# A layer's latent output pair gets a fourth seven-product unit, two of them from kept sums, and two down sets are kept later

## The chip, the cores and the metric

The kernel runs on one core of a Trainium2 chip. The metric is the device time of one execution in microseconds; the median of three runs before the change is 1445.47 us (1445.11 to 1447.64). TensorE (PE) multiplies matrices, VectorE (DVE) and ScalarE (ACT) work element by element, GpSimd (POOL) and SyncE (SP) issue most of the transfers (DMA).

## The reference

One layer of a decoder on 256 tokens of width 2048, all in float32:

```
h = rms_norm(x);  P = h @ w_in                    # queries, latents, keys, values, two gates
A = latent attention (16 heads);  B = sliding-window attention (32 heads)
merged = sigmoid(gA) * (A @ w_o_mla) + sigmoid(gB) * (B @ w_o_swa)
x = x + rms_norm(merged @ w_out)
a, b = split(rms_norm(x) @ ffn_w_up)              # 2 x 5632 columns
x = x + rms_norm((gelu(causal_conv3(a)) * b) @ ffn_w_down)
```

## The kernel before

Every weight is used once, so it is read from memory in pieces of 128x1024 (a row of 128 input features), split and multiplied. A number is kept as a high part `whi` (ScalarE's cast, line 161) and a low part `wlo` (VectorE's subtraction, line 162), and each product is three matmuls: high by high, high by low, low by high (`mm3`, lines 196 to 198). So one piece costs one load on SP's queue into a raw slot, one cast, one subtraction, and its matmuls.

`pair_gemm` multiplies 1024 output columns at a time. It takes the input rows in pairs. A plain pair ("p" in an order string) makes 8 block products, 24 matmuls of 512 columns. A seven-product pair makes 7 (21 matmuls), in the manner of Strassen's and Winograd's scheme: it needs four sums of weight blocks and four sums of activation blocks (`token_sums`, `a_sums`). For "o" the weight sums are made on the spot by four VectorE subtractions (`weight_sums`, line 230). For "s" with `parked` they have been kept: `park_sums` loads the two rows on POOL's queue into a staging tile (line 244), subtracts in four steps (`less`, line 252), stores them to memory (lines 257, 262), and `seven_parked` later loads the sums like any weight. Behind the last seven-product pair `end_sums` adds the product sums up in one ScalarE copy and four VectorE sums (lines 364 to 371).

Time is counted in ticks: `tick()` runs what was put down for this step by `at`, and a piece or two of weights go by per tick. Within this a scheduler sets the order of each engine's instructions by priority; `keep_in_program_order` and `high_priority` bind or lift single ones. Each engine then works through its queue in order.

The stages, with their place in the profile: the first products, sliding-window attention, gates and the sliding-window output; the latent attention (up to 545 us); the latent output, `a_pair` for columns 0 to 1023 (545 to 587 us) and plain products for the rest; `w_pair` and plain products for `w_out` (633 to 709 us); up-projection, a first part of the down-projection, the rest of the up-projection; at last `db` and `dc`, the last down pairs (from 1341 us). In `dc` the second tokens' products of seven pieces are held back to the end. Each finished block of the result passes `z_block`: a sum, a ScalarE square, and a scaling by the norm's gain (line 1523), which may be put off to a later tick. `A_ORDER` is "ppopopop": five plain pairs, three made on the spot. In the latent attention six sets of sums are kept: `tc0` for `dc`, and `ta0` to `ta4` for the first down part. The others are kept in the up-projection's stage.

Of the kernel before, what the change touches and what calls it, by code (L numbers as in the profile page):

```python
# [19 lines left out]
P = 128  # L20
# [20 lines left out]
def trunk_layer(ctx, tc, x, x_cols_in, conv_cols_in, g_mix_post, g_ffn_post, w_in, w_q, w_kv,  # L41
# [136 lines left out]
    def at(t, *fs):  # L178
        steps[max(t, now[0])].extend(fs)
# [56 lines left out]
    def park_sums(name, w, k, c0, place, t0, lead=5):  # L236

        td = [dram.tile([P, 1024], F32, name=f"{name}{i}") for i in range(2)]
        st = []

        def load():
            rows, tag = place(f"{name}s")
            for i in range(2):
                ins = pool.dma_start(rows[i], w[(k + i) * P:(k + i + 1) * P, c0:c0 + 1024])
                if tag not in staged:
                    tc.keep_in_program_order(ins)
            staged.add(tag)
            st.extend(rows[i][:, j * 512:(j + 1) * 512] for i in range(2) for j in range(2))
            st.extend(rows)

        def less(o, x, y):
            tc.keep_in_program_order(vec.tensor_tensor(st[o], st[x], st[y], op=ALU.subtract))

        def even():
            less(0, 1, 0)
            less(1, 3, 1)
            pool.dma_start(td[0], st[4])

        def odd():
            less(3, 3, 0)  # L260
            less(2, 2, 3)
            pool.dma_start(td[1], st[5])

        at(t0 - lead, load)
        at(t0, even)
        at(t0 + 1, odd)
        return td
# [9 lines left out]
    def pair_gemm(name, w, k0, c0, order, act_of, s_of, kind, d, place=None, sums=None, parked=None, held=None, into=None, tied=False, urgent=True):  # L277
# [80 lines left out]
        def end_sums():  # L358
            q1, q5, q7, q6 = q
            d0, d1, d2, d3 = d() if callable(d) else d  # L360

            def first_sums():
                with tc.high_priority(200) if urgent else nullcontext():
                    act.copy(d0, q1)
                    vec.tensor_tensor(d1, d0, q6, op=ALU.add)
                    vec.tensor_tensor(d2, d1, q7, op=ALU.add)

            def more_sums():
                with tc.high_priority(200) if urgent else nullcontext():
                    vec.tensor_tensor(d3, d2, q5, op=ALU.add)  # L370
                    vec.tensor_tensor(d1, d1, q5, op=ALU.add)

            at(now[0], first_sums)
            at(now[0] + 1, more_sums)

        plain_of, seven_of, spot_of = iter(range(n, len(order))), iter(range(n)), iter(range(order.count("s"), n))
        for i, kd_ in enumerate(order):
# [649 lines left out]
        at(t0 + 6, lambda: pt(0), lambda: pt(1))  # L1027
        at(t0 + 7, lambda: pv(0), lambda: pv(1))

    parked_b2.append(park_sums("tc0_", w_down, 24, 1024, stage, now[0] + 7))  # L1030
    parked_a = [park_a(i, stage, now[0] + 13 + 6 * i) for i in range(EARLY)]
    b = now[0] + 2
    for u in range(8):
        if u % 4 == 0:
# [69 lines left out]
            at(now[0] + later + t, load)  # L1104

    as_ = {}
    as_tiles = []

    def a_sums(u):
        if u % 2 == 0:  # L1110
            as_tiles.append(sb(p3, [P, D], f"as{u // 2}", F32R, tag=f"x2_{u // 2}"))
        o = u % 2 * 1024
        tmp = sb(base, [P, 1024], f"at{u}", tag="rx")
        as_[u] = token_sums(at_[u].bitcast(F32), tmp[:, 0:512], tmp[:, 512:1024],
                            as_tiles[u // 2][:, o:o + 512], as_tiles[u // 2][:, o + 512:o + 1024])
# [12 lines left out]
    def a_pair():  # L1128
        halves = [sb(p6, [P, 1024], f"l{n}1", tag="f" + n, bufs=2) for n in "ab"]
        lds = [merge_loads(0, 8), [[x_[:, t * 512:(t + 1) * 512] for x_ in halves] for t in range(NT)]]  # L1130
        for t in range(NT):
            merge_load(*lds[1][t], 1, t, 11)
        gp = sb(p6, [P, D], "araw", tag="gp")
        more_raw[:] = [raw_of, raw_f, raw_of, lambda name: gp[:, 0:1024], raw_of, raw_f, lambda name: gp[:, 1024:2048]]
        c = pair_gemm("a", wo_a, 0, 0, A_ORDER, lambda k, t: (AH(k)[:, t * P:(t + 1) * P], AL(k)[:, t * P:(t + 1) * P]),
                      lambda u: as_[u], 0, ud_place, tied=True)
        more_raw.clear()
        turn.update(raw=0)

        def pair_evac(i):  # L1140
            t, j = divmod(i, 2)
            vec.tensor_tensor(ud_a[i], ud_a[i], c[i], op=ALU.add)
            merged(*lds[j][t], ud_a[i])

        for n_, i in enumerate((0, 2, 1, 3)):
            at(now[0] + n_, lambda i=i: pair_evac(i))
        for p in range(4):
            at(now[0] + 3 + p, lambda p=p: m_cols(p, lds[p // 2]))

    for u in range(NA_):  # L1150
        at(now[0] + 3 * u, lambda u=u: a_sums(u))
    for i in range(4, 12):
        at(now[0] + 36 + 2 * i, lambda i=i: late_loads(i))
    turn_flex("raw")
# [78 lines left out]
    def w_pair():  # L1233
# [10 lines left out]
        for i in range(4):  # L1244
            at(now[0] + i, lambda i=i: pair_evac(i))

    w_pair()
    es4.close()
    es8, p8 = open_pool("p8")
# [320 lines left out]
    def pair_end(i):  # L1570
        t, j = divmod(i, 2)
        vec.tensor_tensor(dsum[t][j], dsum[t][j], ud[i], op=ALU.add)
        z_block(c_db[i], j, t, now[0] + (8 if t == 0 else 14))

    a_raw = lambda k: lambda name: a_tile(name, k)
    more_raw[:] = [raw_of, a_raw(2), raw_of, a_raw(3), raw_of, a_raw(6), a_raw(7)]
# [26 lines left out]
        unpark(i // 4, i % 4)  # L1603
    for i in range(4):
        t, j = divmod(i, 2)
        vec.tensor_tensor(dsum[t][2 + j], dsum[t][2 + j], ud2[i], op=ALU.add)
    z_block(c[0], 2, 0)
    z_block(c[1], 3, 0)
    z_pre(0)
# [24 lines left out]


RING = 4
A_ORDER = "ppopopop"
NA_ = A_ORDER.count("o")
GATE_ORDER = "ppspspsp"
OUT_ORDER = "ppsppspp"  # L1640
B_ORDER = "pospsspssp"
# [76 lines left out]
```

## Time and profile before

| | |
|---|---|
| median of three runs | 1445.47 us |
| the profiled execution | 1445.55 us |
| its span, first to last instruction | 1443.8 us |
| PE busy | 1432.9 us (99%) |
| DVE busy | 1206.8 us (84%) |
| ACT busy | 877.1 us (61%) |
| mean granted clock of TensorE | 0.998 |

Busy times are those of one execution under the profiler. Matmuls overlap: one of 512 columns is shown with 0.39 us, but they follow each other faster, so the pace is read from the starts. VectorE's steps overlap a little as well. A row of the order in time has the start, the length, the engine, the line, what is written and read, and in brackets how long the engine had been idle and who ended that.

### The profile page before, as it was taken

To read this page: it belongs to the slowest core of one execution; us is meant where nothing else is said; L and a number is where in the kernel's file an instruction comes from. 1 tells how busy PE (TensorE), PEld (TensorE's weight loads), DVE (VectorE), ACT (ScalarE), POOL (GpSimd) and SP (SyncE) were. 2 spreads that over 40 slices of the span, in tenths; PEclk is the share of its full clock that TensorE was granted. 3 is DMA by queue.
4 is the path that set the end of the run, shared out by engine and by line. 5 is a ranking of instruction groups with operands and counts; after the bars stand their busy time and mean duration, and the time that the engine had idled before them with its cause. 6 is when DMAs were issued, how large, how long until landed. Compare 5 with 4: busy or idle time off the path is not lost.

```text
span 1443.8 us, 21415 instructions
## 1 busy us (share of the span) xinstructions
PE 1432.9 (99%) x7479; PEld 1225.0 (85%) x7479; DVE 1206.8 (84%) x2106; ACT 877.1 (61%) x1414; POOL 112.7 (8%) x224
## 2 busy tenths in 40 slices
PE   9999999999999999999999999999999999999997
PEld 8888888888888888888888888888888888888886
DVE  7789898988777777979799988987989698877798
ACT  7589875554555655455666555556756465555673
POOL 2001000000000111100000111100000110110000
PEclk9999999999999999999999999999999999999999
DMA  9755475657876777866776999877888889878975
GB/s 309 212 177 154 110 251 199 214 180 227 255 213 205 240 235 264 303 234 220 224 253 210 312 326 329 310 262 236 326 289 316 302 294 305 273 265 279 342 254 215
DMA packets 162315, 365.44 MB, mean 253 GB/s; under 512 B 21008, under 2 KB 32144, under 8 KB 162208
## 3 DMA queue, kind: packets, MB, share of 16 engines
q1 hardware_dynamic: 138192, 278.82, 58.4%
q0 software_dynamic: 23872, 85.00, 17.3%
q8 instruction: 58, 0.95, 0.3%
q14 instruction: 49, 0.40, 0.1%
q10 hardware_dynamic: 144, 0.26, 0.1%
HBM read 327.29 MB, written 36.75 MB: 252 GB/s over the span
## 4 chain that ended last, share of the span: by engine, by line
PE 95%; DVE 2%; ACT 1%; issue 1%; DMA 1%; DVEq 0%; ACTq 0%
PE ub L1407 10%; PE ua L1407 10%; PE accg L196 8%; PE accg L198 8%; PE accg L197 8%; PE ub L1411 5%; PE ua L1411 5%; PE cd L198 2%; PE cd L196 2%; PE cd L197 2%; PE cg L196 2%; PE cg L198 2%; PE cg L197 2%; PE qd L198 1%; PE qd L196 1%; PE qd L197 1%
## 5 line engine op out<-in xcount | busy, mean ns | idle before, releaser
L161 ACT CAST whi<-raw 128x1024 fp32r<-128x1024 f32 (+2 forms) x494 | 497.6, 1017 | 332.7 <-PE accg L198 78.1
L162 DVE TENSOR_TENSOR wlo<-raw,whi 128x1024 fp32r<-128x1024 f32 (+2 forms) x494 | 574.5, 1176 | 119.6 <-ACT whi L161 114.3
L1407 PE MATMUL ua<-ahl,whi 128*128 128x512 f32 x640 | 154.6, 391 | 0.0
L1407 PE MATMUL ub<-ahl,whi 128*128 128x512 f32 x640 | 154.5, 391 | 0.0
L196 PE MATMUL accg<-whi,ahl 128*128 128x512 f32 (+1 forms) x352 | 137.3, 391 | 0.0
L1407 PEld LDWEIGHTS ua<-ahl,whi 128*128 128x128 f32 x640 | 117.6, 188 | 22.7
L1407 PEld LDWEIGHTS ub<-ahl,whi 128*128 128x128 f32 x640 | 117.6, 188 | 22.7
L198 PE MATMUL accg<-whi,ahl 128*128 128x512 f32 (+1 forms) x352 | 136.0, 386 | 0.0
L197 PE MATMUL accg<-wlo,ahl 128*128 128x512 f32 (+1 forms) x352 | 135.5, 385 | 0.0
L1411 PEld LDWEIGHTS ub<-ahl,wlo 128*128 128x128 f32 x640 | 82.2, 191 | 3.2
L1411 PEld LDWEIGHTS ua<-ahl,wlo 128*128 128x128 f32 x640 | 82.2, 191 | 3.1
L1411 PE MATMUL ua<-ahl,wlo 128*128 128x256 f32 x640 | 83.7, 283 | 0.0
L1411 PE MATMUL ub<-ahl,wlo 128*128 128x256 f32 x640 | 83.2, 283 | 0.0
L198 PEld LDWEIGHTS accg<-whi,ahl 128*128 128x128 f32 x352 | 66.1, 188 | 12.6
L196 PE MATMUL accg<-whi,bhl 128*128 128x512 f32 x192 | 76.1, 396 | 0.0
L198 PE MATMUL accg<-whi,bhl 128*128 128x512 f32 x192 | 75.2, 391 | 0.0
L197 PEld LDWEIGHTS accg<-wlo,ahl 128*128 128x128 f32 x352 | 66.2, 188 | 10.4
L197 PE MATMUL accg<-wlo,bhl 128*128 128x512 f32 x192 | 75.1, 391 | 0.0
L196 PEld LDWEIGHTS accg<-whi,ahl 128*128 128x128 f32 x352 | 66.1, 188 | 10.4
L162 DVE TENSOR_TENSOR wlo<-xraw,whi 128x1024 fp32r<-128x1024 f32 x33 | 40.3, 1220 | 12.9 <-ACT whi L161 12.6
L161 ACT CAST whi<-xraw 128x1024 fp32r<-128x1024 f32 x33 | 34.8, 1054 | 24.5 <-PE ub L1407 14.2
L198 PEld LDWEIGHTS accg<-whi,bhl 128*128 128x128 f32 x192 | 36.1, 188 | 7.6
(757 smaller groups left out, 2947.8 us busy)
## 6 DMA issues: line engine op xcount, KB each, us to landing
raw<-in_ffn_w_up_dram SPq DMA_DIRECT2D x143, 512.0 KB, 5.3
raw<-in_w_in_dram SPq DMA_DIRECT2D x99, 512.0 KB, 4.5
raw<-in_ffn_w_down_dram SPq DMA_DIRECT2D x61, 512.0 KB, 6.0
xraw<-in_ffn_w_up_dram SPq DMA_DIRECT2D x33, 512.0 KB, 5.7
ta_s<-in_ffn_w_down_dram POOLq DMA_DIRECT2D x32, 512.0 KB, 6.3
ta<-ta_s POOLq DMA_DIRECT2D x32, 512.0 KB, 5.5
raw<-ta SPq DMA_DIRECT2D x32, 512.0 KB, 5.5
raw<-in_w_o_swa_dram SPq DMA_DIRECT2D x28, 512.0 KB, 4.8
```

What stands on the lines that cost most here:

```text
L161: act.copy(hi[:, a:b], raw[:, a:b])
L162: vec.tensor_tensor(lo[:, a:b], raw[:, a:b], hi[:, a:b].bitcast(F32), op=ALU.subtract)
L196: pe.matmul(o, ah, bh, start=start, stop=False)
L197: pe.matmul(o, ah, bl, start=False, stop=False)
L198: pe.matmul(o, al, bh, start=False, stop=stop)
L1407: pe.matmul(acc[i], hi[:, c], hn[p][:, j * 512:(j + 1) * 512], start=p + j == 0, stop=stop)
L1411: pe.matmul(acc[i][:, 0:256], lo[:, c], hn[p][:, j * 512:j * 512 + 256], start=False, stop=False)
```

## The change

The latent output's pair goes from "ppopopop" to "pposposp": four plain pairs and four seven-product pairs, of which two load kept sums (`parked_w`, made in the latent attention ahead of `tc0`) and two make them on the spot. The token sums of the four are made in the order in which the pairs come. Two of the five early down sets are no longer made in the latent attention but beside `w_pair`. Apart from that, the sums behind the last pair, `dc`, which is the one without `urgent`, come three ticks later and are bound to program order, and the scalings of `db`'s blocks come at 6 and 9 ticks instead of 8 and 14.

```diff
@@ end_sums @@
+            def add(o, x_, y):
+                ins = vec.tensor_tensor(o, x_, y, op=ALU.add)
+                if not urgent:
+                    tc.keep_in_program_order(ins)
...
-            at(now[0], first_sums)
-            at(now[0] + 1, more_sums)
+            at(now[0] + (0 if urgent else 3), first_sums)
+            at(now[0] + (1 if urgent else 4), more_sums)
@@ the latent attention @@
-    parked_b2.append(park_sums("tc0_", w_down, 24, 1024, stage, now[0] + 7))
-    parked_a = [park_a(i, stage, now[0] + 13 + 6 * i) for i in range(EARLY)]
+    parked_w = [park_sums(f"tw{i}_", wo_a, 2 * i, 0, stage, now[0] + 7 + 6 * i) for i in range(2)]
+    parked_b2.append(park_sums("tc0_", w_down, 24, 1024, stage, now[0] + 19))
+    parked_a = [park_a(i, stage, now[0] + 25 + 6 * i) for i in range(EARLY - 2)]
@@ a_pair @@
-                      lambda u: as_[u], 0, ud_place, tied=True)
+                      lambda u: as_[u], 0, ud_place, parked=parked_w, tied=True)
...
-    for u in range(NA_):
-        at(now[0] + 3 * u, lambda u=u: a_sums(u))
+    for u, t in ((2, 0), (0, 3), (3, 6), (1, 9)):
+        at(now[0] + t, lambda u=u: a_sums(u))
@@ the w_out stage @@
+    for i in range(2):
+        parked_a.append(park_a(EARLY - 2 + i, stage, now[0] + 13 + 7 * i))
     w_pair()
@@ the last down pairs @@
-        z_block(c_db[i], j, t, now[0] + (8 if t == 0 else 14))
+        z_block(c_db[i], j, t, now[0] + (6 if t == 0 else 9))
...
-        vec.tensor_tensor(dsum[t][2 + j], dsum[t][2 + j], ud2[i], op=ALU.add)
+        tc.keep_in_program_order(vec.tensor_tensor(dsum[t][2 + j], dsum[t][2 + j], ud2[i], op=ALU.add))
@@ the tables @@
-A_ORDER = "ppopopop"
-NA_ = A_ORDER.count("o")
+A_ORDER = "pposposp"
```

What stands in VectorE's queue before the change where `w_pair` ends: the splits of the last two weight sums (`yg`), of the last plain pair's two rows and of the next columns' pieces (`raw`), and the sums of the pair's products (lines 365 to 371, `qw`).

```order
L162 TENSOR_TENSOR wlo_7102<-yg_1_6407,whi_7101 128x1024
L162 TENSOR_TENSOR wlo_7113<-yg_1_6409,whi_7112 128x1024
L162 TENSOR_TENSOR wlo_7125<-raw_7122,whi_7124 128x1024
L162 TENSOR_TENSOR wlo_7147<-raw_7144,whi_7146 128x1024
L365 TENSOR_TENSOR yg_0_6406<-yg_0_6406,qw_6921 128x512
L162 TENSOR_TENSOR wlo_7173<-raw_7170,whi_7172 128x1024
L366 TENSOR_TENSOR yg_0_6408<-yg_0_6406,qw_6920 128x512
L162 TENSOR_TENSOR wlo_7196<-raw_7193,whi_7195 128x1024
L370 TENSOR_TENSOR yg_0_6408<-yg_0_6408,qw_6919 128x512
L371 TENSOR_TENSOR yg_0_6406<-yg_0_6406,qw_6919 128x512
```

And in the changed kernel, where the sums have line 363 and the subtractions of the first moved down set (`ta_s`) line 252:

```order
L162 TENSOR_TENSOR wlo_7135<-yg_1_6424,whi_7134 128x1024
L252 TENSOR_TENSOR ta_s<-ta_s 128x512
L162 TENSOR_TENSOR wlo_7150<-raw_7147,whi_7149 128x1024
L252 TENSOR_TENSOR ta_s<-ta_s 128x512
L363 TENSOR_TENSOR yg_0_6421<-yg_0_6421,qw_6940 128x512
L252 TENSOR_TENSOR ta_s<-ta_s 128x512
L363 TENSOR_TENSOR yg_0_6423<-yg_0_6421,qw_6939 128x512
L252 TENSOR_TENSOR ta_s<-ta_s 128x512
L363 TENSOR_TENSOR yg_0_6423<-yg_0_6423,qw_6938 128x512
L363 TENSOR_TENSOR yg_0_6421<-yg_0_6421,qw_6938 128x512
L162 TENSOR_TENSOR wlo_7175<-raw_7172,whi_7174 128x1024
L162 TENSOR_TENSOR wlo_7204<-raw_7201,whi_7203 128x1024
```

The split of the last plain row (`raw_7144` before, `raw_7172` now) stood directly behind the one before it; now four subtractions and four sums are between them.

TensorE's queue at the same place in the changed kernel, from the last plain row's first matmul (`whi_7174`, `wlo_7175`) on; `accg` are the next columns:

```order
L196 MATMUL cw_6835<-whi_7174,ahl_6024 128x512
L196 MATMUL cw_6836<-whi_7174,ahl_6024 128x512
L196 MATMUL cw_6837<-whi_7174,ahl_6024 128x512
L196 MATMUL cw_6838<-whi_7174,ahl_6024 128x512
L196 MATMUL accg_0_7199<-whi_7203,ahl_6017 128x512
L196 MATMUL accg_1_7200<-whi_7203,ahl_6017 128x512
L197 MATMUL cw_6835<-wlo_7175,ahl_6024 128x512
L198 MATMUL cw_6835<-whi_7174,ahl_6024 128x512
```

Before, the order there was 196, 197, 198 for each block; now six matmuls that need no `wlo` of this row come ahead of the first that does.

VectorE's queue in `dc` before the change, from the split of a kept sum to the last pieces' splits; `L1523` is a scaling of a `db` block, `L1606` the sum with the pair's product sums (`ue`), `L365` to `L371` these sums:

```order
L162 TENSOR_TENSOR wlo_14425<-raw_14422,whi_14424 128x1024
L1523 TENSOR_TENSOR ds_0_10868<-ds_0_10868,gpost_0_13637 128x512
L162 TENSOR_TENSOR wh_14439<-raw_14436,wh_14438 128x1024
L1523 TENSOR_TENSOR ds_0_10868<-ds_0_10868,gpost_0_13637 128x512
L1606 TENSOR_TENSOR ds_1_11401<-ds_1_11401,ue_14434 128x512
L365 TENSOR_TENSOR ue_14434<-ue_14434,qdc_14153 128x512
L162 TENSOR_TENSOR wlo_14454<-raw_14451,whi_14453 128x1024
L366 TENSOR_TENSOR ue_14435<-ue_14434,qdc_14152 128x512
L162 TENSOR_TENSOR wlo_14468<-raw_14465,whi_14467 128x1024
```

And in the changed kernel (`L1531` is the scaling, `L363` the sums):

```order
L162 TENSOR_TENSOR wlo_14417<-raw_14414,whi_14416 128x1024
L1531 TENSOR_TENSOR ds_0_10905<-ds_0_10905,gpost_0_13674 128x512
L162 TENSOR_TENSOR wlo_14430<-raw_14427,whi_14429 128x1024
L162 TENSOR_TENSOR wlo_14442<-raw_14439,whi_14441 128x512
L162 TENSOR_TENSOR wlo_14451<-raw_14448,whi_14450 128x1024
L1531 TENSOR_TENSOR ds_0_10905<-ds_0_10905,gpost_0_13674 128x512
L162 TENSOR_TENSOR wlo_14464<-raw_14461,whi_14463 128x1024
L162 TENSOR_TENSOR wh_14478<-raw_14475,wh_14477 128x1024
L162 TENSOR_TENSOR wlo_14490<-raw_14487,whi_14489 128x1024
L162 TENSOR_TENSOR wlo_14502<-raw_14499,whi_14501 128x1024
L162 TENSOR_TENSOR wlo_14514<-raw_14511,whi_14513 128x1024
L363 TENSOR_TENSOR ue_14473<-ue_14473,qdc_14190 128x512
```

Behind the split into `wh` the next splits now follow directly; the scalings stand further up, and the first of the sums comes behind three more splits.

## Rows read from the trace of the kernel before

**Rows 1.** The page's head: span; busy us, share of the span and instructions.

```profile
span 1443.8 us, 21415 instructions
...
PE 1432.9 (99%) x7479; PEld 1225.0 (85%) x7479; DVE 1206.8 (84%) x2106; ACT 877.1 (61%) x1414; POOL 112.7 (8%) x224
```

**Rows 2.** PE's waits: whom it waited for, us in total, times, longest.

```profile
PE warm L74 <- DVE ramp L65: 1.1, 1, 1.1
PE cdc L197 <- DVE wlo L162: 0.9, 1, 0.9
```

**Rows 3.** PE in order of time at the end.

```profile
1417.23 0.39 PE L196 MATMUL cdc<-whi,bhl 128*128 128x512 f32 x1
1418.54 0.50 PE L197 MATMUL cdc<-wlo,bhl 128*128 128x512 f32 x1 [0.92 <-DVE wlo L162]
...
1426.47 0.39 PE L198 MATMUL cdc<-wh,bhl 128*128 128x512 f32 x1
...
1434.85 0.28 PE L198 MATMUL zb<-whi,ghl 128*128 128x256 f32 x1
```

**Rows 4.** PE in order of time, the last plain pair of w_pair.

```profile
670.28 0.39 PE L196 MATMUL cw<-whi,ahl 128*128 128x512 f32 x1
...
675.72 0.39 PE L196 MATMUL accg<-whi,ahl 128*128 128x512 f32 x1
```

**Rows 5.** DVE in order of time, start of the latent output's pair.

```profile
547.20 1.23 DVE L162 TENSOR_TENSOR wlo<-araw,whi 128x1024 fp32r<-128x1024 f32 x1 [1.42 <-ACT whi L161]
549.35 1.22 DVE L162 TENSOR_TENSOR wlo<-raw,whi 128x1024 fp32r<-128x1024 f32 x1 [0.92 <-ACT whi L161]
```

**Rows 6.** ACT in order of time, the down pair db.

```profile
1365.75 1.05 ACT L161 CAST whi<-raw 128x1024 fp32r<-128x1024 f32 x1 [1.67 <-PE cdb L198]
```

**Rows 7.** Stretches: length, busy us of PE, PEld, DVE, ACT, POOL; PEclk, DMA share, GB/s.

```profile
545.00:590.00 45.00, 45.00 (x201) 37.25 (x199) 36.90 (x45) 24.10 (x26) 3.85 (x8) 1.00 0.79 276
...
633.00:675.00 42.00, 42.00 (x190) 34.76 (x190) 35.79 (x44) 22.87 (x25) 2.67 (x5) 1.00 0.55 175
675.00:715.00 40.00, 39.95 (x178) 32.79 (x178) 29.80 (x41) 22.39 (x31) 0.07 (x1) 1.00 0.72 236
```

**Rows 8.** DVE in order of time, end of w_pair.

```profile
661.43 0.68 DVE L230 TENSOR_TENSOR yg<-mr3hi 128x512 f32<-128x512 f32 x1
662.03 0.69 DVE L230 TENSOR_TENSOR yg<-mr3lo,mr3hi 128x512 f32<-128x512 f32 x1
...
666.85 1.22 DVE L162 TENSOR_TENSOR wlo<-yg,whi 128x1024 fp32r<-128x1024 f32 x1 [1.20 <-ACT whi L161]
668.21 1.23 DVE L162 TENSOR_TENSOR wlo<-raw,whi 128x1024 fp32r<-128x1024 f32 x1
669.64 1.23 DVE L162 TENSOR_TENSOR wlo<-raw,whi 128x1024 fp32r<-128x1024 f32 x1 [0.20 <-ACT whi L161]
```

**Rows 9.** DVE in order of time at the end.

```profile
1411.30 2.50 DVE L162 TENSOR_TENSOR wlo<-raw,whi 128x1024 fp32r<-128x1024 f32 x2 [0.93 <-ACT whi L161]
...
1414.33 1.22 DVE L162 TENSOR_TENSOR wh<-raw,wh 128x1024 fp32r<-128x1024 f32 x1
...
1417.26 1.22 DVE L162 TENSOR_TENSOR wlo<-raw,whi 128x1024 fp32r<-128x1024 f32 x1
...
1434.99 0.75 DVE L1518 TENSOR_TENSOR z<-ds,zb 128x256 f32<-128x256 f32 x2
```

**Rows 10.** POOL in order of time, latent attention.

```profile
481.14 0.54 POOL L262 DMA_DIRECT2D ta<-ta_s  x1 [3.77 <-DVE ta_s L252]
486.08 1.06 POOL L244 DMA_DIRECT2D ta_s<-in_ffn_w_down_dram  x2 [4.40 <-DMA ta<-ta_s]
```

**Rows 11.** The staging tile's transfers, loads and stores together.

```profile
DMA to landing us min/median/max: 2.9/6.2/8.7
```

**Rows 12.** ACT in order of time, dc.

```profile
1410.22 1.05 ACT L161 CAST whi<-raw 128x1024 fp32r<-128x1024 f32 x1 [1.69 <-DMA raw<-tc]
```

More of the change, by code (lines that the diff above doesn't have):

```diff
@@ L364, in first_sums @@
                     act.copy(d0, q1)
-                    vec.tensor_tensor(d1, d0, q6, op=ALU.add)
-                    vec.tensor_tensor(d2, d1, q7, op=ALU.add)
+                    add(d1, d0, q6)
+                    add(d2, d1, q7)
             def more_sums():
                 with tc.high_priority(200) if urgent else nullcontext():
-                    vec.tensor_tensor(d3, d2, q5, op=ALU.add)
-                    vec.tensor_tensor(d1, d1, q5, op=ALU.add)
-            at(now[0], first_sums)
-            at(now[0] + 1, more_sums)
+                    add(d3, d2, q5)
+                    add(d1, d1, q5)
+            at(now[0] + (0 if urgent else 3), first_sums)
+            at(now[0] + (1 if urgent else 4), more_sums)
         plain_of, seven_of, spot_of = iter(range(n, len(order))), iter(range(n)), iter(range(order.count("s"), n))
@@ L1106, in trunk_layer @@
     as_ = {}
-    as_tiles = []
+    as_tiles = {}
     def a_sums(u):
-        if u % 2 == 0:
-            as_tiles.append(sb(p3, [P, D], f"as{u // 2}", F32R, tag=f"x2_{u // 2}"))
+        if u // 2 not in as_tiles:
+            as_tiles[u // 2] = sb(p3, [P, D], f"as{u // 2}", F32R, tag=f"x2_{u // 2}")
         o = u % 2 * 1024
```

## The prediction

> **What bounds the kernel now.** I read the page's head first: the span is 1443.8 us and TensorE (PE) is busy for 1432.9 us of it [rows 1]. The 10.9 us left are 1.1 us ahead of the first warm-up matmul [rows 2], 0.9 us in one wait on VectorE (DVE) near the end [rows 2], and the 8.7 us behind the last matmul, which starts at 1434.85 us and takes 0.28 [rows 3]. So the second view is PE's waits, which has these two rows and no other [rows 2]: TensorE is the bound from the first product to the last, and any other engine matters only where it makes PE wait. Its pace comes from the order in time: from 670.28 to 675.72 us 24 matmuls of 512 columns start, 0.2267 us each [rows 4]; the one of the wait starts 1.31 us after the one before it [rows 3]. The reader is to see that VectorE, though busy for 84% of the span [rows 1], is paced by PE for nearly all of it: its idle time ends with ScalarE's cast [rows 5], and that cast ends its own wait when PE gives back a weight slot [rows 6].
>
> A change is therefore worth the matmuls it takes away, less the waits it brings to PE, plus what happens in the tail, where PE is done and DVE's queue alone is left.
>
> **The change part by part.**
>
> *One plain pair of rows becomes a seven-product pair.* `A_ORDER` had five plain pairs (24 matmuls each) and three sevens (21); it now has four and four. Three matmuls of 512 columns go: 3 x 0.2267 = 0.68 us [rows 4], all of it on the path, since PE has no gap in this stage (45.00 us busy of 45.00 [rows 7]). Value -0.68; I see no reason for more or less.
>
> *What feeds that stage.* DVE's work in it hardly changes: a seven-product pair costs three subtractions of 1024 columns and one of 512 where a plain one costs two of 1024 (+1.14 + 0.60 us), and a fourth token sum comes (some 2 us: two steps at 0.60 and four small ones at about 0.2), against which the 4 weight sums of one on-spot unit fewer go (4 x 0.60). The fourth token sum is issued between two weight splits, where DVE waits 1.42 and 0.92 us for ScalarE [rows 5]: hidden; without that cover it is 2 us earlier work in a queue that is several microseconds ahead, still nothing. The two kept units now read their sums by DMA through the same seven raw slots. The nearest row is the down stage, which runs kept units through seven slots as well: there the casts wait for PE, not for a DMA [rows 6]. Value 0, bounds 0 to +1.3.
>
> *The attention stage* made six kept sets (one for the last down columns, five down sets) and makes six now (two of `w_o_mla`, that one, three down sets), at the same places of DVE's and POOL's queues, four subtractions, two loads and two stores each. 0.
>
> *Two down sets go into the w_out stage.* This is 8 new subtractions of 128x512 on DVE, 4 loads and 4 stores on the POOL queue. The first set's four land in the worst place, inside the last 10 us of the pair, between the split of the last weight sum and the split of the last plain row. I work it out on the clock of before. That split of the last sum starts at 666.85 and the next can start 1.14 later, at 667.99 [rows 8]. In front of the split of the last plain row there used to be one split; now there are one split, the four new subtractions and all four sums of the pair's products, which the new order puts ahead of it (first two excerpts of the order, in the section on the change): 1.14 + 8 x 0.60 = 5.94 us. The pitch of 0.60 is that of neighbouring 512-column steps, 661.43 to 662.03 [rows 8]. So the split starts at 673.93 instead of 669.64 [rows 8] and ends 1.23 later, at 675.16. PE wants it, in the new order, after 12 matmuls of the row before, four high products and two of the next columns brought forward: 670.28 + 18 x 0.2267 = 674.36 us [rows 4]. It is late by 0.80, with 0.06 us of hand-off (split ends 1418.48, matmul starts 1418.54 [rows 3, 9]) 0.86 us. What a wait costs PE beyond its first gap is seen at the one wait before: the gap is 1.08 us over the pitch, but the 35 matmuls from 1417.23 to 1426.47 take 9.24 instead of 7.93 us, 1.31 in all [rows 3]. By that ratio 0.86 becomes 1.04. Value +1.0. The bounds: with one step less in the way it is +0.3, and PE cannot gain from added work; with eight steps that follow each other at their whole 0.68 us [rows 8], 0.64 us more, it is (0.86 + 0.64) x 1.21 = +1.8.
>
> The Trainium skill (VectorE: DVE Perf Modes, § The DRAIN you can't avoid) says that a VectorE step does not begin until the one before has emptied the pipe. The trace does not agree: steps that take 0.68 us follow each other at 0.60 [rows 8]. By that rule this term would be its upper bound, and the sum +0.7 instead of -0.1 us.
>
> After that the queue recovers: each chunk of the next columns gives PE 12 matmuls, 2.72 us, against 1.14 for its split and 1.2 for two sums, so the second set's four steps, one ahead of each of four later splits, fall into a growing lead. They wait for a load, though: POOL issues it once the first set's store has landed, 4.4 us behind the end of the store's issue, as between 481.14 + 0.54 and 486.08 [rows 10]. From the end of the fourth subtraction, 672.8, that gives a load at 678.3, and with the median landing of 6.2 us [rows 11] its second half at 685.0, against about 685.6 when DVE gets there. Value 0; the upper end is the second rival.
>
> *The sums of the last pair come three steps later, and the scaling of the finished blocks earlier.* Before, three 0.60 us steps (one `L1523`, one `L1606`, one `L365`) stand between the split that ends at 1415.5 and the one that starts at 1417.26, for which PE waits [rows 9]. Now they are out of its way: of the four scalings three come before the gap in which DVE waits to 1411.30 for a late load (0.93 us idle [rows 9]; the cast waited 1.69 us [rows 12]). The split PE waited for can then end at 1416.5 instead of 1418.48, and PE wants it at 1417.46: the wait goes, PE ends 1.31 us sooner. What is late next is DVE: its queue runs densely from there to the last blocks, whose sum starts at 1434.99 [rows 9], while PE's last matmul is over at 1435.13 [rows 3]; so the tail gains only what DVE gains, one 0.60 us step moved into the idle 0.93. Part of that is lost again, because the first two scalings delay the return of raw slots by up to 0.8 us while loads are the limit. Value -0.4; bounds +0.2 and -1.3 (PE's whole gain).
>
> **Sum:** -0.68 + 1.0 - 0.4 = -0.1 us. The profiled execution took 1445.55 us (span plus 1.75), 0.08 above the median; so 1445.5 us.
>
> **The rivals.**
>
> *No new wait, and the whole tail.* If DVE reaches the last plain row in time, 1.0 us is not paid, and if the end follows PE, the tail gives 1.31: -0.68 - 0.6 to -1.31, 1443.6 to 1444.3. For it: the splits of before are ready 2.4 us ahead of PE there (669.64 + 1.23 against 673.23). Against it: 4.3 us are put in front. Chance 0.18.
>
> *The second set's load comes late, and the kernel is slower.* The first of its subtractions waits on DVE for that load, and the split of the sixth chunk of the columns stands behind it; PE wants that at 675.72 + 5 x 2.72 + 0.23, with the 1.0 us of the first wait 690.6 [rows 4]. A store and a load at the longest landing, 8.7 us each [rows 11], put the load at 691.2 and the split's end 1.8 us later, at 693.0: 2.5 us of gap on top, 3.0 by the ratio above, 1448.5. It decides from a landing after 688.7. For it: the landings' spread, 2.9 to 8.7; against it: the median leaves 3.7 us. Chance 0.08.
>
> *Loads short on the raw slots.* The added 4.2 MB share the engines with the weights: 175 GB/s at a share of 0.55 is 318 at full, so 13 us of all engines in a stretch of 40 that is used to 0.72 [rows 7], 11 us free. Splits there are up to 6 us ahead of PE once the columns run, which speaks against it, and two stages would have to fail alike for more. One late raw, its cast as late as the one of [rows 12] (1.69 us) less some 0.4 of lead, is +1.3, in this stage or in that of the latent output: 1446.8. The Trainium skill (DMA: Bandwidth & Descriptors, § Issuing engines are not separate DMA queues) says that transfers of all issuing engines run on the same 16 and interleave; no row here shows how much one queue's landings slow another's. Chance 0.12.
>
> **How the numbers follow.** Forecast 0.62 (its own range 1444.4 to 1446.6), then 0.18, 0.08 and 0.12. A measurement of this kernel tells apart about 0.2%, 2.9 us: faster means under 1442.6, slower over 1448.4. Only the far end of the first rival and a loss that I don't see reach the one: 0.05. The second rival's upper half, and the third together with the forecast's upper bounds, reach the other: 0.09. Same: 0.86. The range, 1443.7 to 1447.6, takes in the first and third rival and leaves out most of the second.
>
> **What would show it.** Right: one wait of PE on a split in the w_out pair near 673 us, 0.7 to 1.0 us; no wait near 1416; three matmuls fewer (7476 records, if none is missing); the pair of the latent output 0.7 us shorter; the tail from the first block's sum to the end unchanged in length, and shorter in all by under 0.7. Wrong: no wait at 673 (first rival); waits at 690 behind a load (second); casts that wait for raw loads while PE stands (third). A time beyond 2.9 us on either side means a mechanism that is not in this list.

## The result, and the profile after

The changed kernel takes 1453.41 us (median of 6 runs, 1452.63 to 1455.12), the kernel before beside it 1445.68 (6 runs, 1444.87 to 1447.70). The ratio is 1.0057, with an interval from 1.0046 to 1.0067: 7.7 us slower. The forecast was 1445.5 us and its range ended at 1447.6; it was wrong.

The head of the page after, where [rows 1] stood before:

```profile
span 1450.8 us, 21452 instructions
...
PE 1434.5 (99%) x7476; PEld 1224.2 (84%) x7476; DVE 1213.8 (84%) x2118; ACT 878.9 (61%) x1417; POOL 116.8 (8%) x232
```

Three matmuls are gone, and yet the span is 7.0 us longer. PE's waits (whom it waited for, us in total, times, longest) say where, against the two rows of before [rows 2]:

```profile
PE accg L197 <- DVE wlo L162: 2.2, 3, 0.8
PE accg L196 <- DVE uda L363: 1.8, 1, 1.8
PE warm L74 <- DVE ramp L65: 1.1, 1, 1.1
PE accg L196 <- ACT whi L161: 0.8, 2, 0.5
PE cw L197 <- DVE wlo L162: 0.6, 1, 0.6
PE x2T L1209 <- DVE x L1206: 0.4, 1, 0.4
PE acckv L197 <- DVE wlo L162: 0.3, 1, 0.3
```

The wait at the end of `dc` is gone. New are one in the latent output (`uda`), the predicted one on a split in `w_pair` (`cw`), and five behind it in the last columns of `w_out` (`accg`), with a short one (`x2T`) after these; the one of 0.3 us (`acckv`) is among the first products. In order of time on PE, with the last matmul, which started at 1434.85 before [rows 3]:

```profile
586.82 0.39 PE L198 MATMUL accg<-whi,bhl 128*128 128x512 f32 x1
588.97 0.50 PE L196 MATMUL accg<-whi,bhl 128*128 128x512 f32 x1 [1.76 <-DVE uda L363]
...
676.79 0.50 PE L197 MATMUL cw<-wlo,ahl 128*128 128x512 f32 x1 [0.63 <-DVE wlo L162]
...
703.92 0.39 PE L198 MATMUL accg<-whi,ahl 128*128 128x512 f32 x1
704.62 0.49 PE L196 MATMUL accg<-whi,ahl 128*128 128x512 f32 x1 [0.32 <-ACT whi L161]
705.88 0.50 PE L197 MATMUL accg<-wlo,ahl 128*128 128x512 f32 x1 [0.77 <-DVE wlo L162]
...
714.84 0.50 PE L197 MATMUL accg<-wlo,ahl 128*128 128x512 f32 x1 [0.68 <-DVE wlo L162]
...
1441.71 0.28 PE L198 MATMUL zb<-whi,ghl 128*128 128x256 f32 x1
```

By the starts the first stall costs 2.15 - 0.23 = 1.9 us, and the one at 676.79 a gap of 1.07, that is 0.84 beyond the pitch. Seven gaps follow between 703.92 and 714.84, in a stretch where PE had stood for 0.05 us of 40 before [rows 7]. The same stretches after:

```profile
545.00:590.00 45.00, 43.24 (x191) 35.48 (x190) 36.83 (x45) 26.33 (x29) 3.77 (x7) 1.00 0.89 314
633.00:675.00 42.00, 42.00 (x190) 34.77 (x190) 35.73 (x45) 22.41 (x26) 3.52 (x7) 1.00 0.56 182
675.00:715.00 40.00, 36.21 (x151) 27.55 (x151) 28.94 (x33) 19.04 (x27) 3.44 (x7) 1.00 0.87 305
```

PE loses 1.76 us in the first and 3.8 in the third, where the engines of the DMA are now busy to 0.87 instead of 0.72. That share looks like the cause; the experiments show that VectorE's added steps bring most of the loss without the sets' own transfers, at a share of 0.76.

The same matmuls in both profiles show where the time goes. The first one of `w_pair` starts at 633.26 us before and at 634.86 after, the first of `ua` in the up stage at 767.45 and 775.57, and PE's last at 1434.85 and 1441.71. An earlier matmul, at 535.79 and 536.01, is 0.22 us apart already; less that, the change is 1.38 us behind at the start of `w_pair`, 7.90 at that of `ua` and 6.64 at the end.

**The stall at 588.97.** `accg` is the second accumulator of the next columns; its bank was one of the pair's and is free when the last two product sums (L363) are done. These two stand on DVE behind a split that waits for a cast:

```profile
586.49 1.23 DVE L162 TENSOR_TENSOR wlo<-raw,whi 128x1024 fp32r<-128x1024 f32 x1 [2.70 <-ACT whi L161]
587.63 1.28 DVE L363 TENSOR_TENSOR uda<-uda,qa 128x512 f32<-128x512 f32 x2
```

and the cast waits on ACT for a load:

```profile
585.41 3.19 ACT L161 CAST whi<-raw 128x1024 fp32r<-128x1024 f32 x3 [4.25 <-DMA raw<-in_w_o_mla_dram]
```

It is the load of the columns' second chunk, the third of the column loads in SP's queue. SP issues it at 578.70, just as the split that empties its slot ends (it starts at 577.45 and takes about 1.23). In SP's order of time:

```profile
578.70 0.37 SPq L140 DMA_DIRECT2D raw<-in_w_o_mla_dram  x1
```

The view by line, cut to this one load, gives its landing:

```profile
DMA to landing us min/median/max: 6.6/6.6/6.6
```

Before the change the same load was issued at 576.78 and landed sooner:

```profile
576.78 0.37 SPq L140 DMA_DIRECT2D raw<-in_w_o_mla_dram  x1
```

```profile
DMA to landing us min/median/max: 4.5/4.5/4.5
```

The slots follow a cycle of seven (`more_raw`). The pair took 22 of them before and takes 24 now, so at its end the cycle stands two places further, and the last pieces sit in other slots. The next columns use only the five of the ring, and find them free later.

### The profile page after: what moved, and what is told of

It reads as the page before. It is cut to its first block, busy times and chain, and to the rows that moved or that the text cites. A ratio compares the mean times of both kernels' runs of the same rounds, so it can differ in the third digit from the quotient of the medians.

```text
span 1450.8 us, 21452 instructions
## 1 busy us (share of the span) xinstructions
PE 1434.5 (99%) x7476; PEld 1224.2 (84%) x7476; DVE 1213.8 (84%) x2118; ACT 878.9 (61%) x1417; POOL 116.8 (8%) x232
## 4 chain that ended last, share of the span: by engine, by line
PE 93%; DMA 3%; DVE 2%; ACT 1%; issue 0%; SPq 0%; DVEq 0%; ACTq 0%
PE ub L1415 10%; PE ua L1415 10%; PE accg L196 7%; PE accg L198 7%; PE accg L197 7%; PE ub L1419 5%; PE ua L1419 5%; DMA raw<-in_w_out_dram 2%; PE cd L196 2%; PE cd L198 2%; PE cd L197 2%; PE cg L198 2%; PE cg L196 2%; PE cg L197 2%; PE qd L196 1%; PE qd L198 1%
```

## The experiments

Each is compared with runs of the kernel before on the same chip (medians 1445.0 to 1445.5). The last column is a length read from each profile: from one and the same matmul near the end of the latent attention (it starts at 535.79 us before and at 536.01 after) to the start of PE's last. What lies ahead of it varies by up to 1.7 us between these profiles and does not enter. It is one execution each, and for e4_up_ring, e5_transfers, e6_subs and e7_one one of the two fastest.

| kernel | median us | ratio [interval] | PE's length us |
|---|---|---|---|
| before | 1445.68 | 1 | 899.06 |
| after | 1453.41 | 1.0057 [1.0046, 1.0067] | 905.70 |
| e1_tail | 1445.67 | 1.0005 [0.9996, 1.0014] | 897.78 |
| e2_up | 1448.73 | 1.0027 [1.0017, 1.0038] | 902.06 |
| e3_ring | 1450.28 | 1.0034 [1.0022, 1.0046] | 903.12 |
| e4_up_ring | 1445.23 | 0.9998 [0.9990, 1.0007] | 897.05 |
| e5_transfers | 1446.44 | 1.0007 [0.9999, 1.0016] | 897.12 |
| e6_subs | 1450.31 | 1.0042 [1.0029, 1.0056] | 901.41 |
| e7_one | 1447.13 | 1.0017 [1.0008, 1.0026] | 899.09 |
| e8_wide | 1458.98 | 1.0096 [1.0082, 1.0110] | 912.10 |
| e9_phase | 1450.77 | 1.0037 [1.0025, 1.0050] | 904.72 |
| e10_old_tail | 1445.23 | 0.9998 [0.9989, 1.0007] | 899.78 |
| e11_pool | 1445.43 | 1.0002 [0.9993, 1.0011] | 898.11 |
| e12_again | 1445.98 | 1.0005 [0.9996, 1.0014] | 897.32 |
| e13_early | 1449.40 | 1.0026 [1.0017, 1.0035] | 901.39 |

**e1_tail: the end's edits alone, on the kernel before.**

```diff
-            at(now[0], first_sums)
-            at(now[0] + 1, more_sums)
+            at(now[0] + (0 if urgent else 3), first_sums)
+            at(now[0] + (1 if urgent else 4), more_sums)
-        z_block(c_db[i], j, t, now[0] + (8 if t == 0 else 14))
+        z_block(c_db[i], j, t, now[0] + (6 if t == 0 else 9))
```

> The kernel before with the edits of the last pair alone (its sums three steps later, the finished blocks scaled earlier). Theory: the wait of TensorE near 1417 us was all that stood between the last loads and the end, so TensorE's last matmul starts 1.3 us sooner and the whole is 1.2 us shorter, 1444.5. As predicted: VectorE's queue sets the end, -0.4 us, 1445.3. If the edits are worth nothing by themselves: 1445.7.

PE's length is 1.28 us shorter, and the wait near 1417 is gone. DVE's last four steps start 2.99 us behind PE's last matmul (2.82 before), so 1.11 of it reaches DVE's end (PE's last starts at 1434.00, DVE's four in this row):

```profile
1436.99 2.74 DVE L1557 SCALAR_TENSOR_TENSOR ds<-ds,rz,x2b 128x512 f32<-128x512 f32 x4
```

The time shows none of it: the interval allows 0.6 us at most. In the profiled execution the slowest of the last stores took 3.2 us to land instead of 2.2, about as much as the gain. Whether that belongs to the edit or to chance is open.

**e2_up: the two sets in the up stage, on the kernel after.**

```diff
-    for i in range(2):
-        parked_a.append(park_a(EARLY - 2 + i, stage, now[0] + 13 + 7 * i))
-    for i in range(sum(NA) - EARLY):
-        parked_a.append(park_a(i + EARLY, second_stage if i % 2 else stage, now[0] + 9 + UP_STEP * i // 2, lead=9))
+    for i in range(sum(NA) - EARLY + 2):
+        parked_a.append(park_a(i + EARLY - 2, second_stage if i % 2 else stage, now[0] + 9 + UP_STEP * i // 2, lead=9))
-UP_STEP = 11
+UP_STEP = 9
```

> The kernel after with its two down sets of the w_out stage made in the up stage instead, with the other eleven (step 9 for 11, so that the last comes at the same place). Theory: these two sets alone make the stalls between 675 and 722 us (1.0 + 5.2 + 0.6), which go; the one at 586.8 (2.1) stays: 1453.4 - 6.8 = 1446.6. Rival, that the late loads of the latent pair carry on into the w_out stage: part of the stalls at 704 to 715 stays, 1448 or more. Rival, that the up stage has no room for 13 sets: new waits there.

Every wait between 675 and 722 us is gone; the one at 587 stays, and this time it is 3.0 us. The up stage takes 13 sets without a wait in this profile. Behind this longer stand PE's granted clock is 0.50 (from 592 to 594 us), and eight matmuls start 0.427 us apart instead of 0.227; against e4_up_ring, which has no such stand, PE's length is 5.01 us longer. The eight runs lie between 1446.3 and 1452.2; that the stall's size makes this spread is likely, but only one of them was profiled.

**e3_ring: the phase of the cycle mended, on the kernel after.**

```diff
-        more_raw[:] = [raw_of, raw_f, raw_of, lambda name: gp[:, 0:1024], raw_of, raw_f, lambda name: gp[:, 1024:2048]]
+        g0, g1 = (lambda name, i=i: gp[:, 1024 * i:1024 * i + 1024] for i in range(2))
+        seven = [raw_of, raw_f, raw_of, g0, raw_of, raw_f, g1]
+        more_raw[:] = seven + seven + [raw_of, raw_f] + seven + [raw_of]
```

> The kernel after with one edit: two entries more in the cycle of raw slots of the latent pair (24 instead of 7 repeated), so that its last two pieces sit in the same slots as before the change and the loads of the next columns find theirs free one or two pieces sooner. Theory: the stall at 586.8 is the phase of that ring; it goes, -2.1 us, 1451.4. Rival, that the kept sums' four more loads or the kept unit itself make the cast late, whatever the slots: the stall stays, 1453.4.

The stall at 587 is gone, PE's length is 2.58 us shorter, and what is left of PE's waits, but for 0.3 us among the first products, is the `w_out` stage:

```profile
PE accg L197 <- DVE wlo L162: 2.0, 3, 0.8
...
PE accg L196 <- ACT whi L161: 0.7, 2, 0.4
PE cw L197 <- DVE wlo L162: 0.6, 1, 0.6
```

But the expectation's reason was half right: the second chunk's load is issued hardly sooner (578.85, in a profile that is 0.65 us later), it lands sooner, in 4.3 us instead of 6.6. Behind it come loads at 579.99 and 582.26; in the kernel after they came at 580.07, 581.49 and 583.23. So the phase spreads the slots' release. That the wider spacing is what makes the load land sooner was not tested apart.

**e4_up_ring: both edits.** The diffs are those of e2_up and e3_ring.

> Both edits together, on the kernel after. Theory: no wait of over 0.5 us is left, and the sum is that of the parts: 1445.7 - 0.7 (three matmuls) - 1.2 (the end) = 1443.8. If one of the stalls has another cause: 1446 to 1447.

PE waits nowhere in the stages that the change touches:

```profile
PE warm L74 <- DVE ramp L65: 1.1, 1, 1.1
PE acckv L526 <- ACT whi L161: 0.3, 1, 0.3
```

Its length is 2.01 us under the kernel before: 0.68 for the three matmuls and 1.28 for the end make 1.96. So the losses are these two and no others. In the order taken here they are 2.58 for the ring's phase and 903.12 - 897.05 = 6.07 for the two sets. In the other order the phase is 902.06 - 897.05 = 5.01 and the sets 3.64, because the stand of e2_up is longer and the clock falls behind it. The median is that of before all the same.

**e5_transfers and e6_subs: the halves of the sets.** Both add to e4_up_ring, in the `w_out` stage, sets whose results nothing reads; the first has only the DMAs, the second only the subtractions, on rows filled by GpSimd.

```diff
+        def load():
...
+                pool.dma_start(rows[k], w_down[(2 * (i + 3) + k) * P:(2 * (i + 3) + k + 1) * P, 0:1024])
...
+        def even():
+            pool.dma_start(td[0], st[4])
+        def odd():
+            pool.dma_start(td[1], st[5])
```

and, in the second:

```diff
+                pool.memset(rows[k], 0.0)
...
+        def even():
+            less(0, 1, 0)
+            less(1, 3, 1)
+        def odd():
+            less(3, 3, 0)
+            less(2, 2, 3)
```

> The kernel without waits (both edits: sets in the up stage, ring phase mended) and, added to it, only the transfers of two down sets in the w_out stage, at the places where the change put them: four loads and four stores of 0.5 MB on POOL's queue, no subtraction (the stores go to a place that nothing reads). Theory: the stalls at 704 to 715 come from loads of w_out that land later beside these transfers, so they are here: +4 to +6, 1449 to 1451; no wait at 675. Rival: VectorE's added steps make them; then this is 1445.2 as without.

> The same kernel without waits and, added to it, only the eight subtractions in the w_out stage, on rows that POOL fills with zeros instead of loading them; no transfer, and nothing reads the results. Theory: the wait of TensorE near 675 us is these steps' (+1.0) and nothing at 704 to 715: 1446.2. Rival: the subtractions delay the weight splits, with them the return of the raw slots and the loads; stalls at 704 to 715, 1449 or more.

The theory of e5_transfers was not put to the test. Its run takes PE's length up by 0.07 us only, but the scheduler, with no subtraction to wait for, put its transfers into the stage before: the last of them goes out at 619.90, where the change has its four stores and the second set's two loads from 672.30 to 697.33. In POOL's order of time, first e5_transfers, then the kernel after:

```profile
619.90 0.54 POOL L1273 DMA_DIRECT2D tx<-tx_s  x1 [1.38 <-DMA tx_s<-in_ffn_w_down_dram]
```

```profile
678.33 1.06 POOL L244 DMA_DIRECT2D ta_s<-in_ffn_w_down_dram  x2 [3.08 <-DMA ta<-ta_s]
```

The stretch from 675 to 715 us says the same, in e5_transfers, e6_subs and e3_ring (the last two numbers are the DMA engines' share and GB/s; e4_up_ring has 0.70 and 234):

```profile
675.00:715.00 40.00, 39.95 (x179) 32.67 (x178) 29.81 (x42) 22.56 (x32) 0.55 (x1) 1.00 0.70 237
```

```profile
675.00:715.00 40.00, 38.33 (x163) 29.93 (x162) 29.56 (x40) 19.78 (x29) 1.08 (x2) 1.00 0.76 255
```

```profile
675.00:715.00 40.00, 36.73 (x153) 28.32 (x154) 28.61 (x32) 18.58 (x27) 3.19 (x6) 1.00 0.87 299
```

So what the transfers alone cost at their place is not known. In e6_subs the subtractions do stand where the change has them, and its theory fell: without the sets' own transfers they cost 4.4 us, bring back both stalls, and lengthen the loads of `w_out` issued between 668 and 700 to a median of 6.7 us, against 4.8 in e4_up_ring. The run is not wholly free of added transfers: the next set's two loads, at 595 in e4_up_ring, go out on POOL's queue at 692.29 and 692.83 here, since the staging tile is in use until then. The first 1.0 us, at 674.61, comes before them; what they add to the rest was not told apart. SP's issues of e6_subs show how. They come at 692.95, 694.04 and 695.18, and the next only after 7 us:

```profile
695.18 0.37 SPq L140 DMA_DIRECT2D raw<-in_w_out_dram  x1
...
702.17 0.37 SPq L140 DMA_DIRECT2D raw<-in_w_out_dram  x1
```

e4_up_ring issues at 687.30, 689.87, 692.21, 694.28 and 696.72, one per chunk. Here the split of the last plain row starts at 673.34 instead of 669.06, 4.3 us later. The slots come back late, three at once, their loads are on the way together and land after 6.8 to 7.0 us, and nothing is issued until these are split. ACT then waits 6.45 us:

```profile
699.84 1.05 ACT L161 CAST whi<-raw 128x1024 fp32r<-128x1024 f32 x1 [6.45 <-DMA raw<-in_w_out_dram]
```

This falls into the columns where only one token tile is multiplied ahead, so PE takes a chunk in 1.36 us instead of 2.72, and the lead is used up at 704. With subtractions and transfers together (e3_ring) it is 1.7 us more, and the rows show the transfers at work: loads that go out at 677.45 and 679.82 in e6_subs land after 7.1 and 6.7 us; those that go out at 677.34 and 679.71 in e7_one, behind the next set's two loads on POOL's queue at 675.98 and 676.50, land after 9.7 and 9.3.

**e7_one: only the first of the two sets.**

```diff
+    parked_a.append(park_a(EARLY - 2, stage, now[0] + 13))
     w_pair()
```

> The kernel without waits with one of the two sets, the first, back in the w_out stage (the other one in the up stage). Theory: the wait at 675 is back (+1.0); the first set's stores and loads are over by 680, so the last columns are fed as before: 1446.2. If one set's transfers are enough to put the raw ring behind: 1448 or more.

PE's length is 2.04 us longer than without: the gap at 673.44 is again 1.07, and one of 0.98 follows at 707.29, one of 0.55 at 715.47. So one set, with its transfers, already delays the last columns; the second adds the other 4.

**e8_wide: five raw slots for the last columns.**

```diff
         last = b == 3
-        if last:
-            flex[0] = "w"
-            turn.update(raw=0, w=0)
...
         if last:
+            turn_flex("w")
             drain()
```

> The kernel after with the ring phase mended (1450.3) and five raw slots instead of three for the last columns of w_out (the two flexible slots stay with the raw loads, the split weights have four instead of five). Theory: three slots at a landing of 6.7 us feed a chunk each 2.2 us at best and so limit the last columns; with five the stalls at 704 to 715 go, -5: 1445.3. Rival: the 16 engines themselves are short; more loads in flight land later and the stalls stay: 1449 to 1451. Rival: four slots of split weights make ScalarE wait for TensorE: new waits there.

Of the seven gaps two are left (0.88 at 705.97 and 2.03 at 714.69), so the three slots were a part of what let the delay through. But the casts of the first `w_up` chunks now stand in ACT's queue ahead of the last block's square and wait there for loads, and the first norm of the residual, which needs it, comes 8 us late:

```profile
PE x2T L1211 <- DVE ry_u L423: 8.1, 1, 8.1
```

**e9_phase: the phase alone, on the kernel before.**

```diff
-        more_raw[:] = [raw_of, raw_f, raw_of, lambda name: gp[:, 0:1024], raw_of, raw_f, lambda name: gp[:, 1024:2048]]
+        more_raw[:] = seven + seven + [raw_of, raw_f, raw_of, g0, g1] + [raw_of, raw_f, raw_of]
```

> The kernel before with one edit: the cycle of raw slots of the latent pair is written out (22 entries) so that its last pieces sit where they sit after the change (plain ring slots instead of the second half of the large slot). Nothing is computed or moved otherwise. Theory: the phase alone makes the first loads of the next columns late, and a stall of 1 to 3.5 us near 587: 1446 to 1448.5. Rival, that the kept units' loads are needed as well: 1445.0, no stall.

The list of slots, and nothing else, costs 5.3 us. The second chunk's load goes out at 579.32 and lands after 7.6 us; PE stands for 3.06 us, and then runs slower:

```profile
587.39 0.39 PE L198 MATMUL accg<-whi,bhl 128*128 128x512 f32 x1
590.84 0.79 PE L196 MATMUL accg<-whi,bhl 128*128 128x512 f32 x1 [3.06 <-DVE uda L371]
591.43 0.63 PE L197 MATMUL accg<-wlo,bhl 128*128 128x512 f32 x1
```

From 591.43 to 596.12 the pitch is 0.427 us. The granted clock of a stretch within (last but two column):

```profile
592.00:594.00 2.00, 2.00 (x7) 1.52 (x6) 2.00 (x4) 0.00 (x0) 0.00 (x0) 0.50 0.25 95
```

**e10_old_tail: e4_up_ring with the end as it was before**, the diff of e1_tail taken back.

> The kernel without waits (sets in the up stage, ring phase mended), with the edits of the last pair undone: sums and scalings at the places they had before. Theory: the wait near 1417 is back, TensorE ends 1.3 us later, the whole is 0.2 to 1.2 us longer: 1445.4 to 1446.4. If the end of VectorE's queue gains nothing from these edits: 1445.2 as without.

The gap near 1418 is back (0.82), and the last 1500 matmuls take 0.77 us more. The median is the same. This profile also loses some 1.9 us in the up stage between 930 and 980, with a gap of 0.75 at 955.67, while ACT waits 5.60 and 2.27 us for loads of `w_up`. The edit does not reach this place, but the stage has two sets more than before.

**e11_pool: the subtractions of the two sets on GpSimd, on e3_ring.**

```diff
-            tc.keep_in_program_order(vec.tensor_tensor(st[o], st[x], st[y], op=ALU.subtract))
+            tc.keep_in_program_order((eng or vec).tensor_tensor(st[o], st[x], st[y], op=ALU.subtract))
-        parked_a.append(park_a(EARLY - 2 + i, stage, now[0] + 13 + 7 * i))
+        parked_a.append(park_a(EARLY - 2 + i, stage, now[0] + 13 + 7 * i, eng=pool))
```

> The kernel after with the ring phase mended, both sets in the w_out stage, and their eight subtractions made by GpSimd (POOL) instead of VectorE; transfers as in the change. Theory: what costs in this stage is VectorE's eight steps, which hold up the splits and with them the return of raw slots and the loads behind; without them on VectorE the waits at 675 and at 704 to 715 go: 1445 to 1446.5. Rival: the sums of the pair, which the new order puts ahead of the last splits, are enough: the wait at 675 stays. Rival: GpSimd's steps slow VectorE's, or are so long that the sets come late.

1445.43: as before the change, and no wait at 675 or 704. It is no clean test, though: in POOL's queue the scheduler put the sets some 50 us earlier, to 616 and 639 us, so that the transfers left the stage along with the subtractions. And they slow DVE there:

```profile
643.76 3.55 POOL L252 TENSOR_TENSOR ta_s<-ta_s 128x512 f32<-128x512 f32 x2
```

```profile
641.63 1.78 DVE L230 TENSOR_TENSOR yg<-mr1lo,yg 128x512 f32<-128x512 f32 x1
643.34 2.81 DVE L162 TENSOR_TENSOR wlo<-yg,whi 128x1024 fp32r<-128x1024 f32 x1
```

A subtraction of 0.68 us takes 1.78 and a split of 1.22 takes 2.81 beside a step of GpSimd, and PE waits once, 0.7 us at 649. The Trainium skill (SBUF — State Buffer, § SBUF: two separate sides) says that DVE steps with two inputs in SBUF and GpSimd's steps take turns at a shared port, each for a whole instruction. These rows agree: DVE's steps grow by 1.1 and 1.6 us, and one of GpSimd takes 1.3 to 1.8.

**e12_again: e4_up_ring once more, unchanged.**

> The kernel without waits once more, unchanged, beside these. Its time was spread from 1443.5 to 1446.5 with a profile at the lower end. If the spread comes from a load that is late in some executions, a profile of a slower one shows a wait of TensorE; else the span grows without one.

The slower execution that was profiled (1446.14) has lost 1.4 us ahead of 535.79, in waits for the first loads (one gap of 1.1 us at 20.13), and 0.3 behind it. So this one lost it in the head, and e10_old_tail in the up stage. The kernels with 13 sets in the up stage and no stall in the profile (e4_up_ring, e5_transfers, e10_old_tail, e12_again) have runs from 1443.4 to 1450.7 us, e1_tail and e11_pool with 11 sets from 1444.7 to 1447.8; whether these sets make the spread is open.

**e13_early: both sets on VectorE, some 60 us earlier, on e3_ring.**

```diff
+    for i in range(2):
+        parked_a.append(park_a(EARLY - 2 + i, stage, now[0] + 6 + 7 * i))
     for j in range(2, 4):
         ld = merge_loads(j)
```

> The kernel after with the ring phase mended and both moved down sets some 16 ticks earlier, in the columns of the latent output, with their subtractions on VectorE as in the change. Theory: eight steps on VectorE cost nothing where the splits are ahead of TensorE and the pace of the next pieces is slow enough to win the lead back; what costs is their place, at the end of the pair and ahead of the last columns. Then no wait at 675 or at 704 to 715: 1445.0 to 1446.0. Rival: the steps cost wherever they stand beside a pair or its columns, and only the move to GpSimd helped: waits elsewhere, 1447 or more.

Neither theory gave this. The first set's steps (609.47 to 613.75) cost nothing, and the waits at 675 and 704 are gone. PE waits 1.2 us at 631 and 2.0 at 638 instead. The second set stands at the head of DVE's queue for 6.86 us, since its load went out at 618.86 only, behind the first set's store:

```profile
618.86 1.06 POOL L244 DMA_DIRECT2D ta_s<-in_ffn_w_down_dram  x2 [3.14 <-DMA ta<-ta_s]
```

```profile
628.70 0.69 DVE L252 TENSOR_TENSOR ta_s<-ta_s 128x512 f32<-128x512 f32 x1 [6.86 <-DMA ta_s<-in_ffn_w_down_dram]
```

So four of VectorE's steps cost nothing at this place; the other four cost because they wait, since with seven ticks between two sets the staging tile's round trip can block the queue.

## Why the prediction was wrong

- *Three matmuls, -0.68*: right; with the end's edits the records give 2.01 us for e4_up_ring, where the two together make 1.96.
- *"What feeds that stage... Value 0, bounds 0 to +1.3"*: this step failed: 2.06 us at its place in the change, 2.58 by e3_ring, 5.0 and more where the stand reaches 3 us (e2_up, e9_phase). The step counted DVE's steps and said that the kept units read "through the same seven raw slots". It did not count the slots: 24 instead of 22 in a cycle of seven shift all that comes behind. e3_ring and e9_phase show that the phase is enough, from both sides. The third rival had the right kind of event, a late raw load in this stage, and the wrong price, because the loss is not the load's own lateness: two product sums queue behind the split, and a bank behind them.
- *The first set, +1.0, by a wait of 0.86 on one split*: the mechanism was right. The split starts at 675.51, where all is 1.59 us later than before, so at 673.92 on the prediction's clock, which had 673.93; the wait is 0.84 and costs 1.0.

```profile
675.51 1.22 DVE L162 TENSOR_TENSOR wlo<-raw,whi 128x1024 fp32r<-128x1024 f32 x1
```

  As the set's whole price it was half: e7_one gives 2.04, the rest at 707 and 715. The section of the Trainium skill that the prediction sets beside this term (VectorE: DVE Perf Modes, § The DRAIN you can't avoid) goes on to say that a step which is not held starts earlier. So the 0.60 us between starts do not contradict it.
- *"After that the queue recovers... Value 0"*: this step failed too, and it is the larger part of the miss: the two sets cost 6.07 us (e3_ring against e4_up_ring), not 1.0, and VectorE's steps without the sets' own transfers 4.4 (e6_subs). It set DVE's 1.14 and 1.2 us per chunk against PE's 2.72 and found a growing lead. It left out that the lead is not DVE's to win: a late split gives its slot back late, and the load behind it takes 4.5 to 7 us, so with three slots the delay goes round the ring (e6_subs) until the last columns, which run at twice the pace, use it up. The second rival named a late load of the set itself; its two loads did land late, after 9.4 and 10.9 us where the rival took 8.7 as the longest, but the step at 688.66 did not wait for them. In e13_early one did.
- *Loads short by the added 4.2 MB*: in part. The stalls come without the sets' own transfers too (e6_subs), so these are not the main cause; with the subtractions they add 1.7 us, and the loads beside them land later. What transfers cost alone at this place is open, since e5_transfers had them some 70 us earlier.
- *The end, -0.4, DVE being late next*: PE's wait went, as said. DVE was hardly late next: its last steps follow PE's last matmul by 2.99 us instead of 2.82, so it gains 1.11; the term was too small. The time of e1_tail has not become shorter; what the last stores do with it is open.

The sum of PE's length: -1.96 (matmuls and end) + 2.58 + 6.07 = 6.69, against 905.70 - 899.06 = 6.64. The forecast's sum had -0.1: it was right in the matmuls and in the first wait, too small in the end, and had put the two other terms at nothing.

No kernel here beats the one before. e4_up_ring keeps the seven-product pair without the losses, e11_pool with 1.0 us of them left (the wait at 649), and both end within 0.1% of it; the 2 us that PE saves in e4_up_ring's records do not show in its median.

## What to carry to other kernels

Count the buffers that an edit takes from a rotating ring: two more in a cycle of seven changed which loads start early, and this alone cost 5.3 us in e9_phase and some 2 in the change. Where few slots feed a stage, price a delay by the whole loop (split, slot, load, cast) up to the next stretch at a faster pace, and not by the first wait: 0.84 us at the first split and its like from the second set became 4.4 to 6.1. A high DMA share beside a stall need not be its main cause; compute steps can be added without their transfers to see, if one looks what else they move. Whatever is added apart, look in the trace whether it stands where the change had it: without the steps that held them back, e5_transfers' transfers ran a stage earlier and tested nothing.

## What the runs showed of the hardware

- Loads of 0.5 MB on SP's queue, one per chunk and 2.1 to 2.6 us apart, landed after 4.3 to 5.0 us (e4_up_ring, 687 to 697). At 1.7 to 2.4 us apart with a load of `x` between and none of POOL's transfers beside them, three others landed after 7.4, 7.1 and 6.7 (e6_subs, 675 to 680); three at 1.1 us apart, behind two loads on POOL's queue, after 6.8 to 7.0 (e6_subs, 693 to 695). Spacing alone does not decide: in e3_ring the load at 578.85, with the next 1.14 us behind, landed after 4.3, and the one at 582.26, 2.27 us behind the one before it, after 8.0.
- The last two of these three in e6_subs (677.45, 679.82) landed after 7.1 and 6.7 us; their like in e7_one (677.34, 679.71) landed after 9.7 and 9.3, where two of the same size had been issued on POOL's queue some 1 to 4 us before.
- After stands of 1.76 us (after) and 2.04 (e13_early) PE went on at full clock (granted 1.00); after one of 3.06 (e9_phase) it ran at the lower of its two levels, 1.2 GHz, for some 13 matmuls, 0.427 us apart instead of 0.227, and after one of 3.04 (e2_up) for eight. In e9_phase that is 2.6 us beyond the wait.
- Beside a subtraction of GpSimd, DVE's steps took 1.78 instead of 0.68 and 2.81 instead of 1.22 us.
